# Sample attention with its 32-column products of four batches side by side in one bank

## The chip, the cores and the metric

One core of a Trainium2 chip runs the whole program. The metric is device time in microseconds for one execution, the median over runs. The engines work in parallel, each in its own order: TensorE (PE, with its weight loads as PEld), VectorE (DVE), ScalarE (ACT), GpSimd (POOL) and SyncE (SP), which here issues all the transfers (DMA).

## The reference

One layer of a decoder for a prompt of 1024 tokens and a sample group of 8 batches with 8 new tokens each, width 1024, all float32:

```
x = x + 1/2 * SwiGLU_1(rmsnorm(x))
h = rmsnorm(x); z = h @ w_in
branch A: windowed attention, 3 groups (window, dilation) = (128,1), (512,4), (2048,16), 4 heads x 64 each
branch B: gated linear recurrence (GeLU gate, width-4 convolution, RG-LRU)
branch C: 4-head cross-attention, head width 128, into 256 memory tokens
merged = sum_b sigmoid(gate_b(h)) * (y_b @ W_b_o);  x = x + merged @ w_out
x = x + 1/2 * SwiGLU_2(rmsnorm(x)); final rmsnorm
```

For the sample tokens branch A reads caches of the last `W` keys and values of each batch. A token sees the cache rows at distances that are multiples of the dilation, so cache rows fall into residue classes: with 8 new tokens 1, 4 and 8 classes are read for the three groups. Branch C reads 256 cached memory keys and values for each batch. A batch has 4 heads x 8 tokens = 32 rows of queries, and that is where the 32 columns come from.

## The kernel before

The **main stream** is matrix products on PE, 128 columns of weights at a time, over three token chunks of 352, 368 and 368. Every weight and activation is split in two `float32r` parts, and `mac3` (L179 to L181) issues three products for each pair. A column tile of `h @ w_in` (`z_tile`) makes 24 such products for each chunk.

The order of the work on PE, ACT, DVE and POOL is written out by hand. Between halves of a chunk's products `tick()` runs one step of the **side work**: generators, in `K.first` and `K.side`, that issue some instructions and then `yield`. A side job gets one step at every second tick; while `hurry` is set (the memory part), one at every tick. So a side step stands in PE's queue between two main products, and everything behind it waits for it. SP's queue holds weight loads (L141), stores of gates (L1094) and the cache loads (L656, L900). PSUM tiles of the side work come from `bank("t")`, two banks.

Three side jobs matter here.

- `mem_sample` attends from the sample tokens into the memory caches, in two halves (`q`) of four batches. For each batch it loads 512 KB of keys (4 KB a partition, tag `mkv`, two buffers), forms the batch's scores with one product per head (L912, 32 columns of `mqz` against 256 memory tokens, accumulated over the four heads: `mqz` is zero outside a head's own rows), and copies them out of PSUM (L914). After a softmax and transposes (L927) it loads each batch's values, multiplies (L940, two products of 512 columns), and masks out the other heads' parts (L942).
- `sample_scores` computes the scores over the window caches on DVE and POOL, from copies of the queries on every partition (`qb`, L675).
- `sample_values` does the softmax and the products with the value caches, for each group `g` and half `q`. `pad` holds the probabilities of each batch and class as 32 columns. Batch by batch it loads the cache rows (`sample_piece`, tag `kv`, three buffers; 4 classes x 1 KB in a row for the larger groups), accumulates one product per class (L755) and one with the new tokens' values (L756, 64 rows) in 32 partitions of a bank, and masks the other heads' parts on the way out of PSUM (L757). The order of the groups is 16, 4, 1.

`sample_mix` then mixes the groups. It writes two halves of 64 columns side by side into one bank (L778):

```
for a in range(2):
    nc.tensor.matmul(ps[a * 64:(a + 1) * 64, :128], self.ogl[:, q, 0, 0:64], self.ident, start=True, stop=True)
```

Around these jobs the prompt's attention (L507, L525, L536) and the recurrent branch (`lru_tile`, with its products L1031 and DVE chain L1020, L1092) run in the same fashion.

Of the kernel before, what the change touches and what calls it, by code (L numbers as in the profile page):

```python
# [39 lines left out]
# rows of w_down taken together, and the width of their column blocks; the last rows stay whole  # L40
DOWN = [(0, 2, 512), (2, 2, 512)] + [(k, 3, 256) for k in range(4, 19, 3)] + [(19, 3, 1024)]
UNITS = [(2, 0), (2, 1), (1, 0), (1, 1), (0, 0), (0, 1)]
# tiles of the gates between the parts of the mixing layer: after the memory heads, after the attention heads,
# after each recurrent tile
FILL = (5, 4, 2)
# the recurrent branch keeps 8 sequences of 8 sample tokens after the prompt, each after 3 tokens of its state
# [4 lines left out]
class Kernel:  # L51
# [8 lines left out]
    def tick(self):  # L60
        """Between halves of a product of the main stream: one step of the work at its side."""
        self.ticks += 1
        for job in [x for x in self.due if x[0] <= self.ticks]:
            self.due.remove(job)
            job[1]()
        if self.first and (self.ticks % 2 or self.hurry):
            try:
                next(self.first[0])
            except StopIteration:
                self.first.pop(0)  # L70
        if self.ticks % 2 == 0 or self.hurry:
            for job in self.side[:2]:
                self.side.remove(job)
                try:
                    next(job)
                    self.side.append(job)
                except StopIteration:
                    pass
# [11 lines left out]
    def banks(self, es, name, **bufs):  # L90
        """Open the PSUM pool of a part of the layer."""
        self.ps = es.enter_context(self.tc.tile_pool(name=name, bufs=1, space=bass.MemoryType.PSUM, reuse_waits="tile"))
        self.ps_bufs = bufs
# [69 lines left out]
    def unit(self, name, w):  # L163
        """The next unit: (j, c) -> both parts of the 128 columns from c of its k-tile j, w columns wide."""
# [36 lines left out]
    # ---- rstd of tokens from the feature-major sums of their squares: token-major first, then as rows on every  # L201
    # partition ----
# [28 lines left out]
    def sumsq(self, k, src, acc, n, eng=None, tag="td"):  # L231
        """Add the squares of one feature tile into acc."""
# [45 lines left out]
    def load_x(self):  # L278
        """The first chunk and weight in small pieces, one after the other."""
# [126 lines left out]
    def toeplitz(self, dst, g, h, col, rows, n):  # L406
        """dst[r, j] = bias row [g, h] at col - r + j."""
        self.nc.sync.dma_start(dst, self.skewed(g, h, col, [[511, rows]], n))
# [29 lines left out]
    def heads(self, g, hp):  # L438
        """q, k and v of one pair of heads; the rest of their work is queued."""
# [40 lines left out]
    def att_job(self):  # L480
        """Prompt attention, three blocks at a time at different stages."""
# [66 lines left out]
    def att_combine(self, pool):  # L548
        """Mix the three head groups of the prompt tokens, 128 at a time."""
# [24 lines left out]
    def mix_groups(self, o, A, H):  # L574
        """o [128, 3, A, H*64 + H + H]: values, -max, sum per head of group g; the mix replaces the values of group 0."""
# [35 lines left out]
    def sample_take(self, g, hp, z):  # L611
        """Keep the sample columns of one pair of heads: token-major, and queries apart by head."""
# [37 lines left out]

    def sample_piece(self, src, g, b, u):
        """[128, n, 256]: rows dil*i + 4u + c of batch b of a cache of group g."""
        dil = GROUPS[g][1]
        n = min(dil, 4)
        t = self.sp.tile([128, 4, 256], F32, name=self.uid("kv"), tag="kv", bufs=3)
        self.nc.sync.dma_start(t[:, :n, :], src[b].rearrange("(i r) f -> i r f", r=dil)[:, 4 * u:4 * u + n, :])  # L656
        return t

    def sample_scores(self, g):
        """Scores of one group over the caches, [cache row, batch, head, token]."""  # L660
# [35 lines left out]
    def sample_values(self, st, g, v_new, qz, k_new):  # L696
        nc, p = self.nc, self.sp
        ncl = min(GROUPS[g][1], 8)
        piece = lambda b, u: self.sample_piece(self.i[f"cache_v{g}"], g, b, u)
# [14 lines left out]
        n2 = -(-ncl // 4)  # L714
        for q in range(2):
# [10 lines left out]
            vts = [piece(q * 4, u) for u in range(n2)]  # L726
# [20 lines left out]
            sel = p.tile([128, 4, 256], F32, name=self.uid("sel"), tag="qb", bufs=2)[:, :, :64]  # L747
            for b4 in range(4):
                cur = vts
                if b4 < 3 and n2 == 1:  # L750
                    vts = [piece(q * 4 + b4 + 1, 0)]
                po = self.bank("t")
                e = slice(b4 * 32, (b4 + 1) * 32)
                for c in range(ncl):
                    nc.tensor.matmul(po[e, :256], pad[:, b4, c, :], cur[c // 4][:, c % 4, :], start=c == 0, stop=False)  # L755
                nc.tensor.matmul(po[e, :256], ptn[:, e], v_new, start=False, stop=True)  # L756
                nc.vector.tensor_tensor(out=sel[e], in0=po[e, :256].rearrange("p (h e) -> p h e", h=4),  # L757
                                        in1=self.dmask[e, :, None].to_broadcast([32, 4, 64]), op=OP.mult)
                if b4 < 3 and n2 == 2:
                    vts = [piece(q * 4 + b4 + 1, u) for u in range(2)]  # L760
                    yield
                yield
            nc.vector.tensor_reduce(og[:, 0:64], sel.rearrange("p h e -> p e h"), axis=AX.X, op=OP.add)
# [23 lines left out]
    def mem_prep(self, mp):  # L787
        """The memory tokens, scaled by the norm's gains and split, and their rstd."""
# [55 lines left out]
    def mem_head(self, h, pool):  # L844
        """One memory head's queries; returns its attention over the prompt as a job."""
# [48 lines left out]
    def mem_sample(self, pool):  # L894
        nc = self.nc
        ck, cv = self.i["cache_mem_k"], self.i["cache_mem_v"].rearrange("b (i k) f -> b i (k f)", k=2)

        def load(src, b):
            t = pool.tile([128, 2, 512], F32, name=self.uid("mkv"), tag="mkv", bufs=2)
            nc.sync.dma_start(t.rearrange("p k f -> p (k f)"), src[b])  # L900
            return t
        kr = load(ck, 0)
        yield
        yield
        for q in range(2):
            s = pool.tile([128, 2, 256], F32, name=self.uid("mss"), tag="mss", bufs=1)
            for b4 in range(4):
                cur, kr = kr, load(ck, q * 4 + b4 + 1) if b4 < 3 else load(cv, q * 4)
                ps = self.bank("t")
                e = slice(b4 * 32, (b4 + 1) * 32)  # L910
                for h in range(4):
                    nc.tensor.matmul(ps[e, :256], self.mqz[:, h, q * 4 + b4, :], cur[:, h // 2, h % 2 * 256:h % 2 * 256 + 256],  # L912
                                     start=h == 0, stop=h == 3)
                nc.vector.tensor_copy(s[e, 0, :], ps[e, :256])  # L914
                yield
# [15 lines left out]
            for b4 in range(4):  # L931
                cur = kr
                if b4 < 3:
                    kr = load(cv, q * 4 + b4 + 1)
                elif q == 0:
                    kr = load(ck, 4)
                po = self.bank("t")
                e = slice(b4 * 32, (b4 + 1) * 32)
                for k in range(2):
                    nc.tensor.matmul(po[e, :], s[:, 1, k * 128 + b4 * 32:k * 128 + (b4 + 1) * 32], cur[:, k, :],  # L940
                                     start=k == 0, stop=k == 1)
                nc.vector.tensor_tensor(out=sel[e], in0=po[e, :].rearrange("p (h e) -> p h e", h=4),  # L942
                                        in1=self.dmask[e, :, None].to_broadcast([32, 4, 128]), op=OP.mult)
# [12 lines left out]
    def lru_constants(self):  # L956
        """4 and -2 softplus(-lambda) by feature, and the recurrent states."""
# [38 lines left out]
    def lru_tile(self, i):  # L996
        """log a = -8 r softplus(-lambda); with t = tanh(-log(a) / 2), sqrt(1 - a^2) = sqrt(t) (1 + a)."""
# [101 lines left out]
    def gate_pair(self, f):  # L1099
        """Two tiles of the gates, chunk by chunk."""  # L1100
# [10 lines left out]
    def merge(self, pool, gates):  # L1111
        """The last chunk first, then the other two with the same weights."""
# [116 lines left out]
    def final(self, c, k):  # L1229
        """Two of the eight parts of a chunk's output."""  # L1230
# [243 lines left out]
def arrange(i):  # L1474
    """The inputs in the layouts that the kernel reads."""
# [22 lines left out]
    a["cache_mem_v"] = i["cache_mem_v"].reshape(NB, NMEM, 512)  # L1498
# [14 lines left out]
def results(o):  # L1513
    """The outputs of reference() from the layouts that the kernel writes."""
# [30 lines left out]
```

## Time and profile before

| | us |
|---|---|
| median of 3 runs | 2857.37 |
| lowest and highest run | 2854.25, 2859.75 |
| span of the profiled execution | 2854.3 |
| PE busy in it | 2801.9 (98%) |
| DVE, ACT, POOL busy | 1309.6, 748.5, 449.0 |

No time of the profiled execution other than its span is given; the span lies 3.1 us under the median of the runs. In rows of the profile, a line such as "L755 PE MATMUL t<-kv,pad 128\*32 128x256 f32 x208" names the source line, engine, operation, the tile written and those read, the used part of the array (rows\*columns), the moving operand and the number of records. A float32 product is two records, a `float32r` product one. Rows of PE overlap, since matmuls are pipelined; the distance between starts tells the pace.

### The profile page before, as it was taken

What the parts mean: (1) busy time and instruction counts of PE and PEld (TensorE: products, weight loads), DVE (VectorE), ACT (ScalarE), POOL (GpSimd) and SP (SyncE); (2) the same over time, 40 slices, a digit from 0 to 9 for tenths busy, and PEclk for the clock granted to TensorE, in tenths of its full rate; (3) what the DMA queues carried; (4) which work ended last, traced back from release to release, by engine and by line L of the source; (5) the groups of instructions that cost most, each with busy time, mean ns of one, the idle gap of its engine ahead of it and who ended that gap; (6) DMA issues with size and microseconds to landing.
All of it is one profiled execution on the core that took longest, in us unless ns stands there. A gap on an engine that the chain in (4) does not pass through costs nothing. (4 is left out here: it accounts for less than half of the span.)

```text
span 2854.3 us, 40939 instructions
## 1 busy us (share of the span) xinstructions
PE 2801.9 (98%) x16762; PEld 2685.4 (94%) x16762; DVE 1309.6 (46%) x2204; ACT 748.5 (26%) x1306; POOL 449.0 (16%) x504
## 2 busy tenths in 40 slices
PE   8999999999999999999989999899999999999998
PEld 7999999999999879999978888899999999999998
DVE  6433333333364433666685445664444333333244
ACT  4112111111253212233334334333321111111112
POOL 3001000000030000112143111332210000000104
PEclk9999999999999999999999999999999999999999
DMA  4222221221243342665544321765222122122121
GB/s 155 78 96 72 84 76 62 84 77 62 77 167 120 97 128 71 186 194 183 169 154 147 120 79 56 255 189 191 89 74 74 67 78 78 67 78 78 67 74 63
DMA packets 142107, 308.03 MB, mean 108 GB/s; under 512 B 17800, under 2 KB 95816, under 8 KB 141248
## 3 DMA queue, kind: packets, MB, share of 16 engines
q1 hardware_dynamic: 141920, 305.42, 32.6%
q8 instruction: 132, 2.16, 0.3%
q14 instruction: 55, 0.45, 0.0%
HBM read 267.97 MB, written 84.19 MB: 123 GB/s over the span
## 5 line engine op out<-in xcount | busy, mean ns | idle before, releaser
L179 PE MATMUL pg<-xg,ws 128*128 128x368 f32 (+1 forms) x2112 | 696.4, 330 | 6.1 <-ACT ws L153 6.1
L181 PE MATMUL pg<-xg,ws 128*128 128x368 f32 (+1 forms) x2112 | 694.4, 329 | 2.0 <-DVE ws L154 2.0
L180 PE MATMUL pg<-xg,ws 128*128 128x368 f32 (+1 forms) x2112 | 690.2, 327 | 0.5 <-DVE xg L199 0.5
L179 PE MATMUL z<-xg,ws 128*128 128x368 f32 (+1 forms) x1392 | 479.4, 344 | 6.0 <-DVE ta L1092 6.0
L181 PE MATMUL z<-xg,ws 128*128 128x368 f32 (+1 forms) x1392 | 457.0, 328 | 0.0
L180 PE MATMUL z<-xg,ws 128*128 128x368 f32 (+1 forms) x1392 | 456.1, 328 | 0.0
L154 DVE TENSOR_TENSOR ws<-wr,ws 128x1024 fp32r<-128x1024 f32 (+2 forms) x257 | 306.8, 1195 | 235.4 <-ACT ws L153 235.2
L179 PEld LDWEIGHTS pg<-xg,ws 128*128 128x128 f32 x2112 | 398.8, 189 | 6.4 <-ACT ws L153 6.1
L181 PEld LDWEIGHTS pg<-xg,ws 128*128 128x128 f32 x2112 | 398.9, 189 | 2.7 <-DVE ws L154 2.7
L180 PEld LDWEIGHTS pg<-xg,ws 128*128 128x128 f32 x2112 | 398.7, 189 | 2.4 <-DVE xg L199 2.4
L153 ACT ACTIVATE ws<-wr 128x1024 fp32r<-128x1024 f32 (+2 forms) x257 | 253.6, 989 | 543.6 <-PE pd L181 373.7
L180 PE MATMUL pd<-h,ws 128*128 128x368 f32 (+1 forms) x1056 | 346.2, 328 | 0.0
L179 PE MATMUL pd<-h,ws 128*128 128x368 f32 (+1 forms) x1056 | 346.0, 328 | 0.0
L181 PE MATMUL pd<-h,ws 128*128 128x368 f32 (+1 forms) x1056 | 345.5, 327 | 0.0
L321 POOL TENSOR_TENSOR td<-sl,tb 128x352 f32<-128x352 f32 (+1 forms) x132 | 128.4, 973 | 1336.7 <-DVE tb L320 1302.9
L179 PEld LDWEIGHTS z<-xg,ws 128*128 128x128 f32 x1392 | 263.2, 189 | 28.2 <-issue 19.0
L348 DVE TENSOR_TENSOR x<-x,pd 128x368 f32<-128x368 f32 (+1 forms) x384 | 199.0, 530 | 189.6 <-PE pd L181 189.5
L180 PEld LDWEIGHTS z<-xg,ws 128*128 128x128 f32 x1392 | 263.4, 189 | 2.8 <-issue 0.3
L181 PEld LDWEIGHTS z<-xg,ws 128*128 128x128 f32 x1392 | 262.8, 189 | 0.0
L320 DVE SCALAR_TENSOR_TENSOR tb<-pg,rbc 128x352 f32<-128x352 f32 (+1 forms) x132 | 70.7, 535 | 316.9 <-PE pg L181 316.9
L179 PEld LDWEIGHTS pd<-h,ws 128*128 128x128 f32 x1056 | 198.3, 188 | 0.0
L181 PEld LDWEIGHTS pd<-h,ws 128*128 128x128 f32 x1056 | 198.3, 188 | 0.0
(267 smaller groups left out, 3145.0 us busy)
## 6 DMA issues: line engine op xcount, KB each, us to landing
wr<-in_w_gu_dram SPq DMA_DIRECT2D x87, 512.0 KB
wr<-in_w_in_dram SPq DMA_DIRECT2D x58, 512.0 KB
qb<-qs_d SPq DMA_DIRECT2D x48, 512.0 KB
out_sk_dram<-in_cache_k_dram SPq DMA_DIRECT2D x16, 1020.0 KB
out_sv_dram<-in_cache_v_dram SPq DMA_DIRECT2D x16, 1020.0 KB
wr<-in_w_dn_dram SPq DMA_DIRECT2D x40, 384.0 KB
kv<-in_cache_k_dram SPq DMA_DIRECT2D x24, 512.0 KB
kv<-in_cache_v_dram SPq DMA_DIRECT2D x24, 512.0 KB
```

The lines of the kernel that those rows point to most:

```text
L153: nc.scalar.activation(spl[:, 0, e], raw[:, e], AF.Copy)
L154: nc.vector.tensor_tensor(out=spl[:, 1, e], in0=raw[:, e], in1=spl[:, 0, e].bitcast(F32), op=OP.subtract)
L179: nc.tensor.matmul(out, wh, xh, start=i == 0, stop=False)
L180: nc.tensor.matmul(out, wh, xl, start=False, stop=False)
L181: nc.tensor.matmul(out, wl, xh, start=False, stop=i == n - 1)
L320: nc.vector.scalar_tensor_tensor(tb, pu[:, :n], 0.5, self.rbc[:, t0:t0 + n], op0=OP.mult, op1=OP.mult)
L321: nc.gpsimd.tensor_tensor(out=td, in0=sl, in1=tb, op=OP.mult)
L348: nc.vector.tensor_tensor(out=xa, in0=xa, in1=ps[:, :n], op=OP.add)
```

## The change

Products are turned from batch by batch into class by class (caches) and head by head (memory). In each step four batches' products stand behind one another in the program, batch `b4` writing the partitions `b4*32` to `b4*32+31` of the same bank. What was accumulated in PSUM over classes or heads is now added in SBUF: the first part is copied by ACT, the others are added by DVE. The mask over heads is applied once for 128 partitions (caches) or as a scalar per partition (memory values, by head). The cache loads follow: `sample_rows` loads one class of four batches with four transfers of 128 KB, two classes ahead; the memory `load` takes one head (keys or values) of four batches, 512 KB in pieces of 1 KB. The new-token products of all four batches follow the last class.

```diff
+    def sample_rows(self, src, g, q, c):
+        t = self.kv_tile()
+        for b in range(4):
+            self.nc.sync.dma_start(t[:, b, :], src[q * 4 + b].rearrange("(i r) f -> i r f", r=GROUPS[g][1])[:, c, :])
+        return t
...
     def sample_values(self, st, g, v_new, qz, k_new):
-            vts = [piece(q * 4, u) for u in range(n2)]
+            vts = [rows_of(q, c) for c in range(min(ncl, 2))]
...
-            sel = p.tile([128, 4, 256], F32, name=self.uid("sel"), tag="qb", bufs=2)[:, :, :64]
-            for b4 in range(4):
-                cur = vts
-                if b4 < 3 and n2 == 1:
-                    vts = [piece(q * 4 + b4 + 1, 0)]
-                po = self.bank("t")
-                e = slice(b4 * 32, (b4 + 1) * 32)
-                for c in range(ncl):
-                    nc.tensor.matmul(po[e, :256], pad[:, b4, c, :], cur[c // 4][:, c % 4, :], start=c == 0, stop=False)
-                nc.tensor.matmul(po[e, :256], ptn[:, e], v_new, start=False, stop=True)
-                nc.vector.tensor_tensor(out=sel[e], in0=po[e, :256].rearrange("p (h e) -> p h e", h=4),
-                                        in1=self.dmask[e, :, None].to_broadcast([32, 4, 64]), op=OP.mult)
-                if b4 < 3 and n2 == 2:
-                    vts = [piece(q * 4 + b4 + 1, u) for u in range(2)]
-                    yield
+            both = p.tile([128, 4, 256], F32, name=self.uid("sel"), tag="qb", bufs=2)
+            acc, sel = both[:, 0, :], both[:, 1, :].rearrange("p (h e) -> p h e", h=4)
+            es = [slice(b4 * 32, (b4 + 1) * 32) for b4 in range(4)]
+            for c in range(ncl):
+                po = self.bank("t")[:, :256]
+                cur, last = vts.pop(0), c == ncl - 1
+                for b4, e in enumerate(es):
+                    nc.tensor.matmul(po[e], pad[:, b4, c, :], cur[:, b4, :], start=True, stop=not last, skip_group_check=True)
+                for e in es if last else ():
+                    nc.tensor.matmul(po[e], ptn[:, e], v_new, start=False, stop=True, skip_group_check=True)
+                if c + 2 < ncl:
+                    vts.append(rows_of(q, c + 2))
+                if c:
+                    nc.vector.tensor_tensor(out=acc, in0=po, in1=acc, op=OP.add)
+                else:
+                    nc.scalar.activation(acc, po, AF.Copy)
                 yield
+            nc.vector.tensor_tensor(out=sel, in0=acc.rearrange("p (h e) -> p h e", h=4),
+                                    in1=self.dmask[:, :, None].to_broadcast([128, 4, 64]), op=OP.mult)
...
     def mem_sample(self, pool):
+            t = pool.tile([128, 4, 256], F32, name=self.uid("mkv"), tag="mkv", bufs=2)
+            a = n % 4 * 256
+            nc.sync.dma_start(t, (ck if n < 4 else cv)[q * 4:q * 4 + 4, :, a:a + 256].rearrange("b p f -> p b f"))
...
+            for h in range(4):
+                cur, kr = kr, load(q, h + 1)
+                ps = self.bank("t")[:, :256]
+                for b4, e in enumerate(es):
+                    nc.tensor.matmul(ps[e], self.mqz[:, h, q * 4 + b4, :], cur[:, b4, :], start=True, stop=True)
+                if h:
+                    nc.vector.tensor_tensor(out=s[:, 0, :], in0=ps, in1=s[:, 0, :], op=OP.add)
+                else:
+                    nc.scalar.activation(s[:, 0, :], ps, AF.Copy)
                 yield
...
+            for h in range(4):
+                cur, kr = kr, load(q, h + 5)
+                po = self.bank("t")[:, :128]
                 for k in range(2):
-                    nc.tensor.matmul(po[e, :], s[:, 1, k * 128 + b4 * 32:k * 128 + (b4 + 1) * 32], cur[:, k, :],
-                                     start=k == 0, stop=k == 1)
-                nc.vector.tensor_tensor(out=sel[e], in0=po[e, :].rearrange("p (h e) -> p h e", h=4),
-                                        in1=self.dmask[e, :, None].to_broadcast([32, 4, 128]), op=OP.mult)
+                    for b4, e in enumerate(es):
+                        nc.tensor.matmul(po[e], s[:, 1, k * 128 + b4 * 32:k * 128 + (b4 + 1) * 32],
+                                         cur[:, b4, k * 128:(k + 1) * 128], start=k == 0, stop=k == 1, skip_group_check=True)
+                nc.vector.tensor_scalar(sel[:, h], po, self.dmask[:, h:h + 1], None, op0=OP.mult)
                 yield
```

Beside this only the layout of the memory values in DRAM changes, so that a head's two halves of rows lie together, and comments go, without a change of line numbers ahead of these functions.

More of the change, by code (lines that the diff above doesn't have):

```diff
@@ L649, in sample_job, with kv_tile @@
         yield from self.sample_mix()
+    def kv_tile(self):
+        return self.sp.tile([128, 4, 256], F32, name=self.uid("kv"), tag="kv", bufs=3)
     def sample_piece(self, src, g, b, u):
@@ L654, in sample_piece @@
         n = min(dil, 4)
-        t = self.sp.tile([128, 4, 256], F32, name=self.uid("kv"), tag="kv", bufs=3)
+        t = self.kv_tile()
         self.nc.sync.dma_start(t[:, :n, :], src[b].rearrange("(i r) f -> i r f", r=dil)[:, 4 * u:4 * u + n, :])
+        return t
+    def sample_rows(self, src, g, q, c):
+        t = self.kv_tile()
+        for b in range(4):
+            self.nc.sync.dma_start(t[:, b, :], src[q * 4 + b].rearrange("(i r) f -> i r f", r=GROUPS[g][1])[:, c, :])
         return t
@@ L698, in sample_values @@
         ncl = min(GROUPS[g][1], 8)
-        piece = lambda b, u: self.sample_piece(self.i[f"cache_v{g}"], g, b, u)
+        rows_of = lambda q, c: self.sample_rows(self.i[f"cache_v{g}"], g, q, c)
         bias_c = p.tile([128, 128], F32, name=self.uid("sbc"), tag="sbc", bufs=1)
@@ L713, in sample_values @@
                                     in1=b8[:, None, :].to_broadcast([128, 8, 8]), op=OP.add)
-        n2 = -(-ncl // 4)
         for q in range(2):
@@ L895, in mem_sample, with load @@
         nc = self.nc
[L896 to L900, printed above, removed]
-            return t
-        kr = load(ck, 0)
+        ck, cv = self.i["cache_mem_k"], self.i["cache_mem_v"]
+        def load(q, n):
+            if n == 8:
+                q, n = q + 1, 0
+            if q > 1:
+                return None
+            t = pool.tile([128, 4, 256], F32, name=self.uid("mkv"), tag="mkv", bufs=2)
+            a = n % 4 * 256
+            nc.sync.dma_start(t, (ck if n < 4 else cv)[q * 4:q * 4 + 4, :, a:a + 256].rearrange("b p f -> p b f"))
+            return t
+        es = [slice(b4 * 32, (b4 + 1) * 32) for b4 in range(4)]
+        kr = load(0, 0)
         yield
@@ L906, in mem_sample @@
             s = pool.tile([128, 2, 256], F32, name=self.uid("mss"), tag="mss", bufs=1)
[L907 to L914, printed above, removed]
+            for h in range(4):
[7 more added lines that the diff above has]
+                    nc.scalar.activation(s[:, 0, :], ps, AF.Copy)
                 yield
@@ L930, in mem_sample @@
             sel = pool.tile([128, 4, 128], F32, name=self.uid("msel"), tag="msel", bufs=1)
[L931 to L938, printed above, removed]
+            for h in range(4):
+                cur, kr = kr, load(q, h + 5)
+                po = self.bank("t")[:, :128]
                 for k in range(2):
-                    nc.tensor.matmul(po[e, :], s[:, 1, k * 128 + b4 * 32:k * 128 + (b4 + 1) * 32], cur[:, k, :],
-                                     start=k == 0, stop=k == 1)
-                nc.vector.tensor_tensor(out=sel[e], in0=po[e, :].rearrange("p (h e) -> p h e", h=4),
-                                        in1=self.dmask[e, :, None].to_broadcast([32, 4, 128]), op=OP.mult)
+                    for b4, e in enumerate(es):
+                        nc.tensor.matmul(po[e], s[:, 1, k * 128 + b4 * 32:k * 128 + (b4 + 1) * 32],
+                                         cur[:, b4, k * 128:(k + 1) * 128], start=k == 0, stop=k == 1, skip_group_check=True)
+                nc.vector.tensor_scalar(sel[:, h], po, self.dmask[:, h:h + 1], None, op0=OP.mult)
                 yield
@@ L1497, in arrange @@
     a["cache_mem_k"] = i["cache_mem_k"].reshape(NB, 128, 2, 4, 128).transpose(0, 4, 3, 2, 1).reshape(NB, 128, 1024)
-    a["cache_mem_v"] = i["cache_mem_v"].reshape(NB, NMEM, 512)
+    a["cache_mem_v"] = (i["cache_mem_v"].reshape(NB, 128, 2, 4, 128).transpose(0, 1, 3, 2, 4)
+                        .reshape(NB, 128, 1024))
     a["state"] = (cat([i["state_conv"].reshape(24, R), i["state_lru"].reshape(8, R)]).T
```

## The prediction

> **What bounds the kernel now.** I read the totals first, then busy time by stretch, then the groups of the products that the change touches, then the timeline around single groups, then the waits.
>
> ```profile
> span 2854.3 us, 40939 instructions
> ...
> PE 2801.9 (98%) x16762; PEld 2685.4 (94%) x16762; DVE 1309.6 (46%) x2204; ACT 748.5 (26%) x1306; POOL 449.0 (16%) x504
> ```
>
> ```profile
> 957.00:1047.00 90.00, 90.00 (x443) 64.85 (x442) 31.66 (x66) 19.29 (x42) 0.00 (x0) 1.00 0.47 144
> 1489.00:1602.00 113.00, 113.00 (x611) 90.16 (x610) 61.60 (x138) 45.18 (x59) 38.06 (x59) 1.00 0.44 137
> 1602.00:1692.00 90.00, 90.00 (x496) 74.95 (x495) 40.42 (x65) 28.33 (x38) 10.67 (x18) 1.00 0.32 107
> 1692.00:1773.00 81.00, 81.00 (x448) 70.13 (x448) 43.83 (x74) 28.52 (x38) 11.10 (x20) 1.00 0.17 58
> ```
>
> The columns of the second view are the stretch, its length, then busy us and instruction counts of PE, PEld, DVE, ACT, POOL, then the granted clock, the DMA share and GB/s. The first stretch holds the memory attention of the sample tokens, the others its products over the value caches, for the groups with 16, 4 and 1 residue classes. In all four PE never rests and its clock is granted in full. Weight loads fall behind PE there (64.85 of 90): something keeps PE busy that isn't the main stream. So whatever PE time the change frees in these stretches shortens the span one for one, until another engine or a load is late.
>
> ```profile
> L755 PE MATMUL t<-kv,pad 128*32 128x256 f32 x208 | 49.4, 382 | 0.0
> ...
> L912 PE MATMUL t<-mkv,mqz 128*32 128x256 f32 x64 | 15.3, 382 | 0.0
> L940 PE MATMUL t<-mkv,mss 128*32 128x512 f32 x32 | 15.2, 598 | 0.0
> ```
>
> Each product uses 32 of 128 columns, and each float32 product is two records: 104 cache products (L755) are x208.
>
> **What these groups cost now.** They sit between main-stream products, so I measure from the start of the last main product before a group to the start of the first behind it, less 0.16, the ordinary distance of two main products (1595.97 to 1596.13).
>
> ```profile
> 1595.97 0.33 PE L180 MATMUL z<-xg,ws 128*128 128x368 f32 x1
> 1596.13 0.33 PE L181 MATMUL z<-xg,ws 128*128 128x368 f32 x1
> 1596.39 3.64 PE L755 MATMUL t<-kv,pad 128*32 128x256 f32 x16
> 1599.96 0.62 PE L756 MATMUL t<-sv,ptn 64*32 64x256 f32 x2
> 1600.51 0.43 PE L179 MATMUL z<-xg,ws 128*128 128x368 f32 x1
> ```
>
> ```profile
> 1667.62 0.32 PE L181 MATMUL z<-xg,ws 128*128 128x352 f32 x1
> 1667.88 1.91 PE L755 MATMUL t<-kv,pad 128*32 128x256 f32 x8
> 1669.72 0.62 PE L756 MATMUL t<-sv,ptn 64*32 64x256 f32 x2
> 1670.27 0.43 PE L179 MATMUL z<-xg,ws 128*128 128x352 f32 x1
> ```
>
> ```profile
> 1016.75 0.33 PE L181 MATMUL z<-xg,ws 128*128 128x368 f32 x1
> 1017.01 1.91 PE L912 MATMUL t<-mkv,mqz 128*32 128x256 f32 x8
> 1018.85 0.44 PE L179 MATMUL z<-xg,ws 128*128 128x368 f32 x1
> ```
>
> ```profile
> 1038.96 0.33 PE L181 MATMUL z<-xg,ws 128*128 128x368 f32 x1
> 1039.22 1.90 PE L940 MATMUL t<-mkv,mss 128*32 128x512 f32 x4
> 1041.05 0.43 PE L179 MATMUL z<-xg,ws 128*128 128x352 f32 x1
> ```
>
> One batch of the 16-class group costs 4.38 - 0.16 = 4.22, of the 4-class group 2.65 - 0.16 = 2.49; eight records make the difference, so a record paces at 1.73 / 8 = 0.216. A batch of memory scores costs 2.10 - 0.16 = 1.94, which is 8 x 0.216 and a fixed 0.21 for going in and out; a batch of memory values 1.93. The product over 64 rows adds 0.12 (2.49 - 10 x 0.216 - 0.21). By these the 1-class group costs 4 x 0.216 + 0.21 + 0.12 = 1.19. Now: 8 x (4.22 + 2.49 + 1.19) = 63.2 us for the caches and 8 x (1.94 + 1.93) = 31.0 for the memory, 94.2 in all.
>
> **What side by side is worth.** One place of this kernel already writes two column halves of a bank next to each other, L778 (64 columns each, 128 moving columns, two products for each half).
>
> ```profile
> 1795.06 0.66 PE L778 MATMUL t<-ident,ogl 128*64 128x128 f32 x8 [2.24 <-POOL ogl L598]
> 1795.64 0.43 PE L179 MATMUL z<-xg,ws 128*128 128x352 f32 x1
> ```
>
> ```profile
> 969.52 0.60 PE L872 MATMUL t<-ident,mp 128*128 128x128 f32 x4
> 969.95 1.03 PE L880 MATMUL s<-mk,qm 128*128 128x256 f32 x4
> ```
>
> L872, in one place of the array, needs 0.43 for four records of 128 columns: 0.1075 each. Eight would take 0.86 one after the other; L778 reaches the next main product after 0.58, with about 0.14 of that for going in and out (0.58 - 4 x 0.1075 = 0.15). So its eight records ran as four pairs. The two passes of a product stand one behind the other in the compiled program, and a strict order would have given five rounds (first pass; second pass beside the neighbour's first; and so on): 5 x 0.1075 + 0.14 = 0.68, a tenth above what the row shows. So a pass that waits for its own columns does not hold up the neighbour's. That four such lanes go as well as two is not shown here; I take four, since nothing in these rows marks two as a limit.
>
> With four lanes a class of four batches (eight records) is two rounds: 2 x 0.216 + 0.21 + 0.02 (estimated, for three staggered starts) = 0.66. Caches: 13 classes x 2 halves = 26 steps x 0.66 = 17.2. The new-token products of four batches now come once per half and group: 6 x (0.432 + 0.02 + 0.12) = 3.4. Memory scores: 8 steps x 0.66 = 5.3. Memory values: sixteen records of 128 columns in four rounds, 4 x 0.1075 + 0.23 = 0.66, 8 of them: 5.3. After: 31.2. **PE is freed of 94.2 - 31.2 = 63.0 us.** If the sixteen small records are limited by issue to half of that, it costs 8 x 0.43 = 3.4 more; I take 0, from L778's pace, and keep 3.4 for the range.
>
> **What else it edits, and its cover.**
>
> ```profile
> PE z L179 <- DVE ta L1092: 6.0, 2, 5.6
> PE g L1031 <- ACT lA L1032: 4.7, 1, 4.7
> PE o L536 <- ACT pt L526: 3.2, 2, 1.8
> PE t L778 <- POOL ogl L598: 2.2, 1, 2.2
> PE g L1031 <- DVE xc L1020: 0.2, 1, 0.2
> ```
>
> ```profile
> L755 PEldq EVENT_SEMAPHORE  x24: 51/51/124, 1487.4 to 1766.7; - x24
> ```
>
> ```profile
> L656 SPq DMA_DIRECT2D kv<-in_cache_v_dram x32: 327/333/480, 1442.3 to 1752.8; - x32
> ```
>
> ```profile
> DMA qb<-qs_d: 163.1, 19
> ```
>
> ```profile
> 1010.84 4.40 SPq L900 DMA_DIRECT2D mkv<-in_cache_mem_k_dram  x2
> ```
>
> ```profile
> L757 DVE TENSOR_TENSOR sel<-t,dmask 32x256 f32<-32x256 f32 x24 | 10.1, 420 | 41.8 <-PE t L756 41.5
> ```
>
> The first five rows are all the waits of PE from 950 to 1800 us (in total, times, longest): none is for a cache load.
>
> *Value loads.* The bytes stay; 32 transfers become 104 (four for each class and half), in pieces of 1 KB where the larger groups had 4 KB. 72 more issues x 0.33 = 24 us of SP's queue over 280 us; behind them on that queue stand the weight loads and the stores of gates. SP has the room: today it waits for PE to free cache buffers. A class is fetched two steps ahead; a step has two ticks, 24 main products, 24 x 0.16 = 3.9, so 3.9 + 0.66 = 4.5 afterwards and 9.1 us of lead. The nearest row is the query copies of the score phase, also 512 KB in 1 KB pieces: their users waited 163.1 / 19 = 8.6 us each, with issue and the wait for a buffer in it. I take no stall. The DMA share, 0.44 at most in the cache stretches, becomes about 0.55 with the same bytes in less time.
>
> *Waits on PE.* A class now waits for four transfers in place of one. With all landed that costs nothing, as the 16-record group, which already takes its second piece in mid-run, paces like the 8-record one. If each extra wait cost 0.05 of the sequencer, as the 24 waits in the row above take, it would be 26 x 3 x 0.05 = 3.9 us. If one is late, the whole main stream queues behind it.
>
> *Memory loads.* Same number and size, two buffers, fetched one step ahead. The load issued at 1010.84, once a buffer was free, feeds the group at 1017.01: 6.17 us of lead, and PE had no wait, so it lands within that. Afterwards the lead is 6.17 - (1.94 - 0.66) = 4.9. A stall lies between 0 and 1.28 in each of the 12 steps that have no softmax ahead, 0 to 15 us. I take 1: the share of 0.47 in that stretch leaves the DMA idle for half of the 6.17, which speaks for the low end, but not for all twelve.
>
> *Evacuations.* One for each class in place of one for each batch, over 128 partitions in place of 32. DVE loses 24 x 0.42 of L757 and the memory's like ones, and gains 20 + 6 adds and 6 masks over 256 elements, at 0.42 each by the same row if cost goes by elements in a partition (13.4 us) and 16 small masks; ACT gains 8 copies. Near zero, all beside PE. But the same DVE work falls into less time: 61.6 us in 113 - 22 = 91 in the first cache stretch, 68%. The two larger waits above are of the kind that grows then (main products waiting for DVE and ACT to read their banks). None today falls in the three cache stretches; a repeat of both would be 10.7. I take 2.
>
> *Order.* The side job has 4 + 1, 4 + 4, 4 + 8 steps for a half in place of 8, 8, 11: 50 against 54, each on every second tick. It ends earlier, and nothing is lost there.
>
> **Sum.** 63.0 - 1 - 2 = 60.0. The profiled execution spans 2854.3 and would span 2794.3; the median shown, 2857.37, lies 3.1 above that span, so I forecast 2797.4.
>
> [...]
>
> **Rivals.**
> 1. *Only two lanes at once.* A class takes four rounds, 1.09; 26 x 1.09 + 6 x 0.99 + 16 x 1.09 = 51.7 after, 42.5 freed, less 3: 2818. For it: only pairs are seen. Against it there is no row, only that the pairs show no sign of a limit.
> 2. *Strict order of passes.* Five rounds for a class (1.08 + 0.24 = 1.32), 1.20 for new tokens, nine short rounds for memory values (1.22): 26 x 1.32 + 6 x 1.20 + 8 x 1.32 + 8 x 1.22 = 61.9, 32.3 freed, less 3: 2828. Against it: L778.
> 3. *No overlap,* because the lanes now read four different moving tiles where L778's halves read the same one. The records stay: (256 + 64) x 0.216 + 128 x 0.1075 + 42 x 0.21 + 6 x 0.12 = 92.4, 1.8 freed: 2856, no change.
> 4. *Slower: class loads come late.* Every step waits in PE's queue for the last of four transfers, which SP issues behind weight loads and stores. The gain is gone at 63.0 / 42 = 1.5 us a step, so when a load takes over 9.1 + 1.5 us; at 2 us a step the time is 2857.4 + 84 - 63 = 2878. Against: 8.6 us, waits included, in the nearest row.
>
> **How the numbers follow.** Chances: forecast 0.70, with its stalls at 0 to some 10; forecast's lanes but waits at their bounds (15 + 10.7 + 3.9 + 3.4 in place of 3, so 2827) 0.06; rival 1 0.08, rival 2 0.06, rival 3 0.05, rival 4 0.05. The forecast's own range is 2792 to 2808; with the bounds and rivals 1 and 2 it is 2791 to 2829, which leaves out about 1 in 10 and a little at each end. Under 0.2% (5.7 us, about what a measurement of this kernel can tell from no change) only rival 3 falls: faster 0.90, same 0.05, slower 0.05.
>
> **What would show it.** Groups of eight cache records taking about 0.8 us from first start to last end in place of 1.91, and 0.66 between main products beyond the ordinary distance; x26 such groups; the value stretch 1489 to 1773 about 43 us shorter, the memory stretch 957 to 1047 about 20. Rounds of five or four show as 1.32 or 1.09. Late loads show as PE waits with cache tiles as releaser, a crowded DVE as more waits of L179 and L1031. The forecast is wrong if such waits pass some 10 us, or if eight records still take over 1.5 us.

## The result, and the profile after

| | before | changed |
|---|---|---|
| median of runs, us | 2858.56 (4 runs, 2854.25 to 2862.20) | 2795.14 (4 runs, 2794.55 to 2796.55) |
| span of the profiled execution, us | 2854.3 | 2793.0 |

The ratio is 0.9775 (95% interval 0.9761 to 0.9789): faster, by 63 us. The forecast was 2797.4, and 2794.3 for the span. Of all the runs named below one, a repeat of the changed kernel (3345 us, at a granted clock of 0.75), fell into a slower state and is not counted. The changed kernel's totals:

```profile
span 2793.0 us, 41227 instructions
...
PE 2740.8 (98%) x16858; PEld 2663.2 (95%) x16858; DVE 1301.2 (47%) x2204; ACT 754.1 (27%) x1316; POOL 442.1 (16%) x504
```

PE is busy for 61.1 us less where the span is 61.3 shorter, and its share stays at 98%: the time came out of PE's own queue. The stretches of the memory attention and of the three cache groups (columns as in the prediction; the boundaries are set by eye):

```profile
957.00:1028.00 71.00, 71.00 (x547) 61.17 (x546) 27.92 (x66) 19.99 (x45) 0.00 (x0) 1.00 0.59 182
1470.00:1552.00 82.00, 82.00 (x534) 71.37 (x533) 52.95 (x131) 42.56 (x58) 35.34 (x50) 1.00 0.51 156
1552.00:1628.00 76.00, 76.00 (x492) 68.50 (x491) 44.10 (x70) 30.33 (x41) 10.64 (x23) 1.00 0.44 141
1628.00:1692.00 64.00, 64.00 (x418) 57.36 (x417) 33.13 (x55) 29.34 (x40) 9.78 (x17) 1.00 0.27 86
```

90 us became 71, and 113 + 90 + 81 = 284 became 222, about 19 and 62 less. (The 62 holds more than the groups, since a boundary set by eye can move some us of main stream.) PE rests in none of them, and weight loads now keep closer to it: 61.17 of 71 where it was 64.85 of 90. Single steps on the timeline, with the main products around them: one class of four batches, a last class with the new tokens, a head's memory scores and a head's memory values.

```profile
1483.79 0.33 PE L181 MATMUL z<-xg,ws 128*128 128x368 f32 x1
1484.05 0.64 PE L763 MATMUL t<-kv,pad 128*32 128x256 f32 x8
1484.61 0.43 PE L179 MATMUL z<-xg,ws 128*128 128x368 f32 x1
...
1507.64 0.33 PE L181 MATMUL z<-xg,ws 128*128 128x368 f32 x1
1507.90 0.64 PE L763 MATMUL t<-kv,pad 128*32 128x256 f32 x8
1508.47 0.64 PE L765 MATMUL t<-sv,ptn 64*32 64x256 f32 x8
1509.03 0.44 PE L179 MATMUL z<-xg,ws 128*128 128x368 f32 x1
```

```profile
1004.30 0.33 PE L181 MATMUL z<-xg,ws 128*128 128x368 f32 x1
1004.56 0.64 PE L930 MATMUL t<-mkv,mqz 128*32 128x256 f32 x8
1005.13 0.43 PE L179 MATMUL z<-xg,ws 128*128 128x368 f32 x1
...
988.48 0.33 PE L181 MATMUL z<-xg,ws 128*128 128x368 f32 x1
988.74 0.64 PE L956 MATMUL t<-mkv,mss 128*32 128x128 f32 x16
989.31 0.43 PE L179 MATMUL z<-xg,ws 128*128 128x368 f32 x1
```

Measured as in the prediction (from main start to main start, less the ordinary distance), a class costs 0.66, a class with new tokens 1.23, a head's scores 0.67 and its values 0.67. The means of each kind, over the steps that stand between two main products, are 0.659, 1.224, 0.659 and 0.662. (For the scores these are three of the eight steps; the others stand behind products of another length.) Eight records that took 1.91 us now take 0.64. All waits of PE from 950 to 1760 us:

```profile
PE z L179 <- DVE ta L1107: 5.2, 1, 5.2
PE g L1046 <- ACT lA L1047: 4.9, 1, 4.9
PE po L179 <- ACT ys L1144: 4.5, 2, 2.4
PE o L536 <- ACT pt L526: 3.6, 3, 1.6
PE po L180 <- DVE ys L1145: 1.6, 2, 0.9
```

No row has a cache tile as its releaser, the two large ones are those of before at about the same size, and the one of 2.2 for `ogl` at L778 (now L790) is gone. The `po` waits belong to the merge, behind the side work. The way from the prompt's first product with the memory keys (L880, now L892) to the merge's first product is 64.0 us shorter (854.7 us, was 918.7), from there to the end 2.4 longer (1048.5, was 1046.1). Within it, the way from the first product with the value caches to the merge's first product is 45.0 us shorter (272.6, was 317.6). A second trace of the changed kernel, `changed_again`, has 852.7, 1050.2 and again 272.6: the first two numbers move by some 2 us between executions of one kernel, the last does not.

### The profile page after: what moved, and what is told of

It reads as the page before. It is cut to its first block, busy times and chain, and to the rows that moved or that the text cites. A ratio compares the mean times of both kernels' runs of the same rounds, so it can differ in the third digit from the quotient of the medians.

```text
span 2793.0 us, 41227 instructions
## 1 busy us (share of the span) xinstructions
PE 2740.8 (98%) x16858; PEld 2663.2 (95%) x16858; DVE 1301.2 (47%) x2204; ACT 754.1 (27%) x1316; POOL 442.1 (16%) x504
## 4 chain that ended last, share of the span: by engine, by line
PE 92%; DVE 3%; DMA 2%; ACT 1%; issue 1%; SPq 0%; POOL 0%; DVEq 0%; ACTq 0%; POOLq 0%
PE pg L179 12%; PE pg L181 12%; PE pg L180 12%; PE z L179 8%; PE z L181 7%; PE z L180 7%; PE pd L180 6%; PE pd L179 6%; PE pd L181 6%; PE po L181 2%; PE po L180 2%; PE po L179 2%; PE o L536 1%; PE wo L179 1%; PE wo L181 1%; PE wo L180 1%
```

## The experiments

Two theories stood at first. A: four column lanes run at the same time, and a step lasts as long as its longest lane. B: the gain comes from elsewhere in the change (fewer and larger evacuations, other transfers, the order of steps). Later runs ask how the lanes run, and what the terms of the sum costed at nothing are worth. In kernels with other numbers of lines the same products stand at other lines (L764, L766, L957).

**One lane.** As the changed kernel, but all four batches write partitions 0 to 31, one after the other. The adds and copies behind them cover those 32 partitions alone, POOL clears the tiles first, and the output of the other partitions is left out. This is the line that matters:

```diff
-es = [slice(b4 * 32, (b4 + 1) * 32) for b4 in range(4)]
+es = [slice(b4 % 1 * 32, b4 % 1 * 32 + 32) for b4 in range(4)]
```

> The changed kernel, but all four batches' products write the same 32 partitions (the output of the sample attention is left out for the other partitions, which stay at zero). Loads, steps, copies and record counts are those of the changed kernel. Theory A (the time comes from four column groups running at the same time): a class of eight records costs 8 x 0.216 + 0.21 = 1.94 us instead of 0.66, memory values 16 x 0.1075 + 0.21 = 1.93, so the gain is gone: 2853 to 2861 us. Theory B (the time comes from what lies around the products: fewer waits of SP for cache buffers, other load pieces, one copy for four batches): it stays near 2795 to 2800 us.

**Two lanes.** The same with `b4 % 2 * 32`, and 64 partitions.

> As one_lane, but with two column groups of 32, two batches in each (half of the sample attention's output is left out). Theory A, rounds set by the longest lane: a class takes four rounds, 4 x 0.216 + 0.23 = 1.09 us, the new tokens' products 0.99, memory values 1.09: 51.7 us in all against 31.2 of the changed kernel, so 2815 to 2820 us. Theory B: near 2795 to 2800 us.

One lane: 2856.91 us, ratio 0.9987 (0.9978 to 0.9997). Two lanes: 2816.44, ratio 0.9844 (0.9829 to 0.9859). A class in each, one lane first:

```profile
1520.71 0.33 PE L181 MATMUL z<-xg,ws 128*128 128x368 f32 x1
1520.96 1.91 PE L764 MATMUL t<-kv,pad 128*32 128x256 f32 x8
1522.81 0.44 PE L179 MATMUL z<-xg,ws 128*128 128x368 f32 x1
```

```profile
1504.32 0.33 PE L181 MATMUL z<-xg,ws 128*128 128x368 f32 x1
1504.58 1.06 PE L764 MATMUL t<-kv,pad 128*32 128x256 f32 x8
1505.56 0.44 PE L179 MATMUL z<-xg,ws 128*128 128x368 f32 x1
```

The means are 1.934 and 1.076, against 0.659 with four lanes. Less the 0.21 for going in and out, that is 1.72, 0.87 and 0.45: eight, four and two rounds of 0.216. With one lane the loads, the number of adds and copies and the order of steps are those of the change (an add takes 0.41 us over 32 partitions and 0.42 over 128), and all but about 4 us of its gain is gone. So B explains no more than these 4.

**Halves of the change.** `caches_only` has the memory part of before, `memory_only` the cache part of before.

> The change in the products with the value caches alone, the memory attention as before. Theory A: 63.2 - 20.6 = 42.6 us gained, so 2813 to 2818 us, and the stretch of memory attention as long as before. If instead the loads by class cost something that the memory part gives back, it is above 2820.

> The change in the memory attention alone, the products with the value caches as before. Theory A: 31.0 - 10.6 = 20.4 us gained, so 2836 to 2841 us, no wait of PE for a memory load. If the shorter steps ran into the loads (lead of 4.9 us), up to 15 us of it would be missing: 2841 to 2856.

2817.22 (ratio 0.9843, 0.9828 to 0.9858) and 2839.77 (0.9926, 0.9911 to 0.9941). Against the 2860.49 of before on the same chip that is 43.3 and 20.7, together 64.0, which is the whole within the spread of the runs: the halves don't help or hinder each other. One part of an expectation failed: `memory_only`, whose memory loads are those of the changed kernel, has a wait for one.

```profile
PE t L918 <- DMA mkv<-in_cache_mem_k_dram: 0.3, 1, 0.3
```

**Lane after lane.** In the memory values a lane's four records (two products of two passes) stand one behind the other, before the next lane's.

```diff
-for k in range(2):
-    for b4, e in enumerate(es):
+for b4, e in enumerate(es):
+    for k in range(2):
```

> The changed kernel with another order of the memory value products in a step: all four records of a batch's lane one behind the other, then the next batch's, instead of alternating batches. Theory A, each lane has its own order and the others run past a lane that is busy: 0.66 us a step as before, time within 0.2% of the changed kernel's 2795. Strict program order: the next lane's first record can only go beside the last record of the lane before, 4 + 3 x 3 = 13 rounds, 13 x 0.1075 + 0.23 = 1.63 us a step, 8 steps, so 7.8 us more: 2801 to 2805. A window that sees only the next one or two products would lie between.

2795.08 (ratio 0.9774, 0.9761 to 0.9788), as the changed kernel.

```profile
988.29 0.33 PE L181 MATMUL z<-xg,ws 128*128 128x368 f32 x1
988.55 0.66 PE L956 MATMUL t<-mkv,mss 128*32 128x128 f32 x16
989.14 0.44 PE L179 MATMUL z<-xg,ws 128*128 128x368 f32 x1
```

A step costs 0.68 to 0.69 where it cost 0.66. With starts in the order of the source a lane could begin only behind the fourth record of the lane before, 4 + 3 x 3 = thirteen rounds in all, 13 x 0.1075 + 0.23 = 1.63. In the trace the single records start in four groups of four, the groups 0.11 to 0.13 us apart and the records of a group 13 ns (7 ns in the changed kernel, so another order did reach PE). So here a lane's first record started 13 ns behind the neighbour's first, while three records of the neighbour that stand ahead of it in the source had not started yet.

**Row counts mixed.** In a last class each batch's product over 128 rows is followed at once by its new-token product over 64 rows.

```diff
 for b4, e in enumerate(es):
     nc.tensor.matmul(po[e], pad[:, b4, c, :], cur[:, b4, :], ...)
-for e in es if last else ():
-    nc.tensor.matmul(po[e], ptn[:, e], v_new, ...)
+    if last:
+        nc.tensor.matmul(po[e], ptn[:, e], v_new, ...)
```

> The changed kernel, but in the last class of a half each batch's product over 128 rows is followed at once by its product over 64 rows (new tokens), instead of four of the one and then four of the other. The 0.12 us of such a change from 128 to 64 rows was measured between two groups. If each change empties the array, lanes can't overlap across it: four times (0.43 + 0.12 + 0.43) + 3 x 0.12 + 0.21 = 4.5 us instead of 1.22, 6 such steps, so 15 to 20 us more: 2810 to 2816. If the lanes keep their own order across the change: 1.0 to 1.3 us a step, no difference.

2816.49 (ratio 0.9847, 0.9834 to 0.9860). Six steps went from 1.224 to 4.469, 19.5 us in all, which is most of the loss of 21.

```profile
1508.98 0.33 PE L181 MATMUL z<-xg,ws 128*128 128x368 f32 x1
1509.24 0.62 PE L763 MATMUL t<-kv,pad 128*32 128x256 f32 x2
1509.79 0.62 PE L765 MATMUL t<-sv,ptn 64*32 64x256 f32 x2
1510.33 0.62 PE L763 MATMUL t<-kv,pad 128*32 128x256 f32 x2
...
1513.62 0.44 PE L179 MATMUL z<-xg,ws 128*128 128x368 f32 x1
```

Each product starts 0.55 behind the one before, two records (0.43) and 0.12: with the row count changing at each product, no lane overlapped another. The 0.12 is what a change added here, and the lost overlap comes on top.

**One transfer for each class.** One of 512 KB in place of four of 128 KB, in the same 1 KB pieces.

```diff
-for b in range(4):
-    self.nc.sync.dma_start(t[:, b, :], src[q * 4 + b].rearrange("(i r) f -> i r f", ...)[:, c, :])
+self.nc.sync.dma_start(t, src[q * 4:q * 4 + 4].rearrange("b (i r) f -> i r b f", ...)[:, c])
```

> The changed kernel with one transfer of 512 KB for a class of four batches in place of four of 128 KB (same 1 KB pieces, 26 transfers in place of 104). The prediction costed the 72 more issues on SP at nothing. If that is right, the time is within 0.2% of the changed kernel's 2795 and PE has no wait for a cache load in either. If SP's queue did hold something up, it is faster by up to some 5 us.

2795.93 (ratio 0.9777, 0.9763 to 0.9790): no difference that these runs can tell. In the changed kernel the issues of the value loads and the waits on PE ahead of the classes read

```profile
L666 SPq DMA_DIRECT2D kv<-in_cache_v_dram x104: 327/430/1466, 1422.9 to 1640.5; - x104
```

```profile
L763 PEldq EVENT_SEMAPHORE  x26: 51/51/51, 1468.3 to 1687.6; - x26
```

(Lowest, median and highest duration in ns, first and last start.) Added up, the 104 issues take 47 us of SP, where the prediction's 0.33 for each gives 34, and SP has them to spare. Each of the 26 steps shows one semaphore event of 0.05, and the steps cost 0.66 with it.

**One buffer for the memory loads.** The load of the next head is issued behind a step's products in place of before them, and can't start until those are done.

```diff
-t = pool.tile([128, 4, 256], F32, ..., tag="mkv", bufs=2)
+t = pool.tile([128, 4, 256], F32, ..., tag="mkv", bufs=1)
...
-cur, kr = kr, load(q, h + 1)
+cur = kr
...                                   # behind the step's products
+kr = load(q, h + 1)
```

> The changed kernel with one buffer for the memory caches in place of two: the next head's load starts when the products of the step before have read the buffer, and has one tick of main work, some 2.1 us, to land, where the changed kernel leaves 4.8 and had no wait. It measures how much of the 4.8 was needed. The prediction bounded the landing at 6.17 us and took 1 us of stall in all. If a load of 512 KB needs 4.5 us or more from issue to use, PE waits 2.4 us or more in each of 12 to 15 steps: 2824 us or more, and the changed kernel was near its edge. If it needs 3.5, PE waits 1.4: 2812 to 2818, and the margin was over 1 us. If the loads were hidden anyway, 2795.

2811.47 (ratio 0.9832, 0.9818 to 0.9847), 16 us slower than the changed kernel, at waits that before and after don't have:

```profile
PE t L957 <- DMA mkv<-in_cache_mem_v_dram: 9.0, 6, 2.0
PE t L930 <- DMA mkv<-in_cache_mem_k_dram: 6.8, 4, 2.3
```

Nine of the ten late loads take 3.5 to 4.0 us from their issue to the first product that needs them, and the first one 5.3. The changed kernel issues its closest loads 4.6 to 4.8 us ahead (one at 1002.5 for the step at 1007.3), and in the stretch of the 5.3 it has 7.0. So these loads had 0.6 to 1.3 us in hand. Not every load in every execution does: in `memory_only` a load with such a lead took 5.3 us (issued at 1003.37 for the step at 1008.65), and that is its wait of 0.3. The term that was to decide between 0 and 15 us is 0 in both traces of the changed kernel, but it is near its edge.

**Two classes in one step.** A better version, if going in and out of the main stream is what is left: two classes are accumulated in the bank, and an empty step follows, so that the loads keep their pace. At the start three classes are loaded ahead in place of two.

```diff
-for c in range(ncl):
+for c in range(0, ncl, 2):
...
+    for j in range(min(2, ncl - c)):
+        cur = vts.pop(0)
+        for b4, e in enumerate(es):
+            nc.tensor.matmul(po[e], pad[:, b4, c + j, :], cur[:, b4, :], start=j == 0, ...)
```

> The changed kernel with two classes in one step (accumulated in the bank), and an empty step behind each, so that the rate of loads stays. Each step into a side group and out of it costs 0.21 us besides the records, and some 0.1 in the first main product behind it. 12 groups fewer: 12 x (2 x 0.66 - (4 x 0.216 + 0.23)) + 12 x 0.1 = 2.7 + 1.2 = 3.9 us gained, 2789 to 2793. Against it: only one class is loaded ahead in full, the second has 8 us from issue to use; if it comes late, PE waits some us in each of 12 steps, and the time is 2795 to 2815.

2791.79 (ratio 0.9759, 0.9746 to 0.9773).

```profile
1490.25 0.33 PE L181 MATMUL z<-xg,ws 128*128 128x368 f32 x1
1490.51 1.07 PE L766 MATMUL t<-kv,pad 128*32 128x256 f32 x16
1491.51 0.44 PE L179 MATMUL z<-xg,ws 128*128 128x368 f32 x1
```

Two classes cost 1.09 where they cost 2 x 0.66, and no load is late. Twelve such steps save 12 x 0.23 = 2.7 us, and twelve first main products behind a step lose their delay of 0.11. The way from the first product with the value caches to the merge is 269.1 us, 3.5 less, where 3.9 were expected. The same pair of kernels again, beside each other:

> The changed kernel again, beside the version with two classes a step: 2793 to 2797 us.

> Two classes a step again, on the same chip as the changed kernel: 3 to 5 us under it, if the 3.9 us worked out from the costs of going in and out of a side group are right; no difference if the lower time before was that of another chip or run.

The changed kernel: 0.9773 (0.9760 to 0.9785), five runs from 2792.46 to 2797.24 with a median of 2794.08. In pairs: 0.9763 (0.9750 to 0.9776), 2791.85 (2789.13 to 2793.13). So pairs are 2 to 3 us faster here, a little under the 3 to 5 that were expected. The intervals overlap, and what is sure is the 3.5 us, which each of the two traces of pairs shows against each of the two of the changed kernel. It is the fastest version that was run, by either count.

## Why the prediction was right

The forecast gain was 60.0 us. It came out at 61.3 by the spans and at 63.4 by the medians. PE was to be freed of 63.0, and was freed of 63.1 in the changed products: the mechanism and its sizes were right, and what was wrong lies in the 3 us of stalls.

*Cost now.* The reading of 94.2 us held: with one lane the same records cost the same again (1.93 a class).

*Cost after.* 0.66, 1.23 with new tokens, 0.66 and 0.66 were forecast; 0.659, 1.224, 0.659 and 0.662 came. By these the groups take 20 x 0.659 + 6 x 1.224 + 8 x 0.659 + 8 x 0.662 = 31.1 us (31.2 forecast). The step from two lanes to four, the one thing that no row of before showed, held, and so did the forecast that four different moving tiles cost nothing (0.659, with 0.66 forecast). No row or run that the forecast names shows its 0.02 for staggered starts; in the changed kernel the four records of a round start 7 ns apart, 0.02 from the first to the last. The issue of sixteen small records at nothing held too (0.662 for a head's values, with 0.66 forecast).

*The rivals.* Two lanes would have given 2818; the kernel that has two gave 2816. Strict order is refuted by the lane-after-lane run (0.68 to 0.69 a step, where strict order gives 1.63). The prediction's own case against it was circular: the 0.14 for going in and out of L778 had been worked out by taking off four rounds, and so could not decide between four and five. Its conclusion held all the same, since the eight single records of L778 start in four pairs (at 1795.06, 1795.22, 1795.33 and 1795.44). No overlap, 2856 in the rival, gave 2857 when it was brought about. Late class loads (2878) needed loads of over 10.6 us by the lead of 9.1 that the prediction took; the lead is longer, 10.8 or more from the last issue of a class to its first product, and there is no wait for any. (Its price counts 42 steps, but class loads feed only 26.)

*The stalls.* Here the sum was wrong, and that the span came within 1.3 us of the forecast is partly luck. The memory loads were put at 1, and cost 0. The crowded DVE was put at 2, and did not come: its share in the first cache stretch did rise (52.95 of 82, 65%, where 68% was forecast), but the two large waits for DVE and ACT stayed as they were, 10.1 together after 10.7. (Of the 16 small masks that it counts for DVE there are 8.) The wait of 2.2 for `ogl`, which the prediction lists, went away, and the sum has no term for that: the 45.0 us gained between the first value product and the merge are about the 63.2 - 17.2 - 3.4 = 42.6 forecast for these products and this 2.2. Against all this, 2.4 us (4.0 in the second trace) were lost where the prediction did not look, in the merge behind the side work. It looked at waits in the three cache stretches and the memory's, and took the rest of the trace as unchanged. PE's waits for `ys` there, 1805 to the end before and 1740 to the end after:

```profile
PE po L179 <- ACT ys L1129: 3.1, 2, 2.3
PE po L180 <- DVE ys L1130: 1.8, 2, 0.9
```

```profile
PE po L179 <- ACT ys L1144: 4.5, 2, 2.4
PE po L180 <- DVE ys L1145: 1.6, 2, 0.9
```

and the stretch at a lower granted clock behind them, before, after, and in `caches_only`:

```profile
1814.40:1817.80 3.40, 3.40 (x13) 3.10 (x12) 3.05 (x4) 2.48 (x3) 0.00 (x0) 0.51 1.06 381
```

```profile
1746.20:1756.30 10.10, 7.33 (x24) 6.46 (x23) 5.80 (x6) 4.73 (x5) 0.00 (x0) 0.50 0.95 306
```

```profile
1766.00:1779.70 13.70, 9.52 (x29) 8.65 (x30) 7.17 (x8) 4.73 (x5) 0.64 (x1) 0.50 0.87 287
```

PE had its clock at half for 3.4 us before and for 10.2 after, and for 13.7 in the second trace of the same changed kernel. All eleven traces of kernels with the new cache part have 10.2 or 13.7 there, among them the one with one lane, as slow as before (10.2). The two with the old cache part have 3.4 and, in `memory_only`, 6.8. So the length does not go with the gain; it may go with the cache half, but two traces on that side are few. The time from the merge's first product to the end goes with it: 1046.1 and 1045.7 us at 3.4 and 6.8, 1047.6 to 1049.4 at 10.2 (nine traces), 1050.1 and 1050.2 at 13.7. What sets the length stays open.

## What to carry to other kernels

Products that use 32 columns cost here as many rounds as their longest lane has records (eight, four and two, at 1.93, 1.08 and 0.66 us for a class): spread independent ones over the four column groups of one bank, and pay for it with adds on an engine that has room. Keep products of the same row count together: with a change of it at each product no lane overlapped another, and a last class took 4.47 us, where it took 1.22 with one change. Once the rounds are short, going in and out of the main stream (0.21 us of 0.66) is the next thing to share, by longer side steps, as long as the loads keep their lead.

## What the runs showed of the hardware that was not expected

The overlap held in both orders of the lanes' records that were run: a step of sixteen records cost 0.68 us lane after lane, and 0.66 interleaved. Changing between 128 and 64 rows at each product made the sixteen records of a last class take 3.7 times as long (4.47 against 1.22).

The half-clock stretches at the merge came in lengths of 3.4, 6.8, 10.2 and 13.7 us, all whole multiples of 3.4. In the traces of before and after, the 3.4 us ahead of the stretch were at a granted clock of 1.00 and not idle throughout: PE was busy for 0.72 of 3.40 us (1742.7 to 1746.1) after, and for 1.74 of 3.41 (1811.1 to 1814.5) before. So here 3.4 us in which PE was half busy could be followed by the half clock. What sets the length of these stretches, no run here isolates.
